# A decoder step in fp32: the second half's layer norm takes its squares about a pivot, during the output projection

## The chip, the cores and the metric

The kernel runs on one core of a Trainium2 chip. The metric is device time in microseconds of one execution, as the median of several; lower is better.

## The reference

One step of a decoder layer for 512 prompt tokens, 16 meta tokens and 8 sample tokens, model width 2048, all in float32. After an input layer norm, one projection gives queries, keys, values and a pooling input; windowed attention and causal pooling give 2048 mixed channels per token. Then:

```python
def layer_norm(x, g, b):
    mu = mean(x); var = mean((x - mu) ** 2)
    return (x - mu) * rsqrt(var + 1e-5) * g + b

mix = concat(attn_out, pool_out) @ w_o
h1  = layer_norm(ALPHA * h + mix, ln1_g, ln1_b)      # the layer norm of this change
a   = silu(h1 @ w_gate) * (h1 @ w_up)                # 44 tiles of 128 columns each
out = layer_norm(ALPHA * h1 + a @ w_down, ln2_g, ln2_b)
```

## The kernel before

**Layout.** After the attention, activations lie with channels on the 128 partitions and tokens along the free axis. The 520 tokens (8 sample, 512 prompt) are two halves of HN = 260. A value of model width is 16 blocks of 128 channels; two blocks of one half make a tile of 128 x 520, named by `k2` from 0 to 7.

**Products of split numbers.** Most matmuls take a weight as a sum of a high and a low part (fp32r) and an operand likewise, and form three products: high by high, high by low, low by high (lines 203, 204, 206). A weight is split in pieces of 128 x 512: ScalarE makes the high part (line 187), VectorE the low part (line 188). Five pieces can be held at once in this stage (`WB`). These two operations are given a priority 400 steps ahead of their place in the program (`WPRIO`).

**Output projection.** `out_proj(h)` runs over the 16 column blocks `m` of w_o for one half `h`. Each takes 48 products and four splits. Then VectorE adds ALPHA times the residual (line 858) and adds the result to `zs`, the running sum of the blocks (line 862). The result `z1[h][k2]` stays in memory.

**Layer norm.** `ln1(h, zs)` is a generator that is advanced step by step between other work. The mean over channels is one matmul of `zs` with a matrix `onesd` that holds 1/2048 everywhere (line 878), so every partition gets the sum. ScalarE copies it (line 880). Then VectorE subtracts the mean from every tile (line 892) and ScalarE squares it.

- For half 0 the squares are added on VectorE into one tile `ss` (lines 897 to 901) and two matmuls sum that over the channels (line 911). This half's norm runs beside the second half's output projection.
- For half 1 each of the 16 blocks of squares goes straight to the array, which sums them in 16 matmuls (line 888).

`rstd_of` makes the reciprocal root with one refining step (lines 238 to 244): VectorE and ScalarE in turn. Then `norm` multiplies (line 920), applies gain and offset on ScalarE (line 923) and stores h1 (line 925). For half 1, lines 934 to 949 form the differences and high and low parts (lines 871, 872) that the gate and up products need.

**Fills.** Gate and up are formed by a seven-product scheme over 2 x 2 blocks, whose first products need only half 0. While half 1's norm runs, the array takes 14 such products in plain f32, eight matmuls each (`ahead`, line 1009). Four stay in the accumulator banks; ten are copied out into the `fill` ring, a ring of five tiles of 128 x 520 (`NF`).

**Order.** A planner chooses each engine's order from a simulated timeline and the priorities. Where the code says `step(pe)`, the array's order is fixed as written: here the first half of fill 0, the mean, the second half of fill 0, the variance, and then the other fills. The steps of `rstd_of` have a priority 600 steps ahead (`LP`); so do the first nine norm steps beside the fills. Loads of weights and stores of h1 are issued from SP's queue. A fill's load needs one of five raw buffers, so it is issued when the fill five back is done.

The loop around the change, from the kernel before:

```python
    for f in (fills[0], g1, fills[0], g1):
        with step(pe):
            next(f)
    for j, f in enumerate(fills[1:]):
        with tc.high_priority(LP if j < 9 else 0):
            next(g1, None)
        with step(pe):
            for _ in f:
                pass
```

Of the kernel before, what the change touches and what calls it, by code (L numbers as in the profile page):

```python
# [8 lines left out]
F32 = mybir.dt.float32  # L9
F32R = mybir.dt.float32r  # L10
AF = mybir.ActivationFunctionType
ALU = mybir.AluOpType
AX = mybir.AxisListType

P = 128
D = 2048
# [8 lines left out]
HN = NTOK // 2  # L25
# [10 lines left out]
EPS = 1e-5  # L36
# [3 lines left out]
NF = 5  # L40
NKEEP = 2
LP = 600
# [25 lines left out]
def hybrid_step(ctx, tc, xin, w_in, w_o, w_g, w_u, w_d, w_pool, par_d, cst_d, ident_d, ln2gb, kct_d, vc_d, hist_d,  # L68
                ck_d, cv_d, sp_d, yp, ys, nkp, nvp, npp, nks, nvs, nps):
    nc = tc.nc  # L70
# [69 lines left out]
    bufs = {"raw": NRAW, "row": 16}  # L140
    par = cp.tile([P, NPAR], F32, name="par")
    onesd = cp.tile([P, P], F32, name="onesd")
# [9 lines left out]
    def row_tile(name, w=NTOK):  # L152

        return ap_.tile([P, NTOK], F32, tag="row", name=name, bufs=bufs["row"])[:, :w]
# [53 lines left out]
    def full_block(src, name, out, hi, lo, low=None, apart=False, side=None):  # L208


        def mm(w, g, js):
            for kk in range(4):
                k = g * 4 + kk
                sl = slice(kk * P, (kk + 1) * P)
                products([out[j] for j in js], w[0][:, sl], w[1][:, sl], [hi(k)[j] for j in js], [lo(k)[j] for j in js],
                         k == 0, k == KT - 1)
                if side is not None:
                    next(side)

        js = list(range(len(out)))  # L220
        ws = []
        for h in range(2):
            raw = load_raw(src[:, h * 1024:(h + 1) * 1024], f"{name}_{h}")
            for g in range(2):
                ws.append(split(raw[:, g * 512:(g + 1) * 512], f"{name}_{h}{g}", low))
                mm(ws[-1], 2 * h + g, js[:1] if apart else js)
        if apart:
            for g in range(4):
                mm(ws[g], g, js[1:])

    def rstd_of(pool, var, n, name):

        w = var.shape[-1]
        if w < HN:
            ve, r, t = [pool.tile([P, NS], F32, tag=f"rs{i}", name=f"rs{i}_{name}", bufs=3)[:n, :w] for i in range(3)]
        else:
            ve, r, t = [pool.tile([P, HN], F32, tag="r" if i == 1 else "t", bufs=1 if i == 1 else NT) for i in range(3)]
        nc.vector.tensor_scalar(ve, var, EPS, None, op0=ALU.add)
        nc.scalar.activation(t, ve, AF.Sqrt)
        nc.vector.reciprocal(r, t)  # L240
        nc.vector.tensor_mul(t, r, r)
        nc.vector.tensor_mul(t, t, ve)
        nc.vector.tensor_scalar(t, t, -0.5, 1.5, op0=ALU.mult, op1=ALU.add)
        nc.vector.tensor_mul(r, r, t)
        return r
# [5 lines left out]
    def stats_end(pool, st, mv, n, name):  # L251
        nc.vector.bn_aggr(mv[:n], st[:n].rearrange("p a b -> p (a b)"))
        return mv[:n, 0:1], rstd_of(pool, mv[:n, 1:2], n, name)
# [3 lines left out]
    with ExitStack() as sa:  # L257
# [185 lines left out]
        for h in range(2):  # L443
            for g in range(4):
                n = h * 4 + g + 1
# [27 lines left out]
            with step(*three):  # L473
                for i in range(4):
                    if i % 2:
                        nc.vector.tensor_scalar(zkv[i][:, XH[h]], out[i], par[:, PBIAS + i:PBIAS + i + 1], None,
                                                op0=ALU.add)
# [339 lines left out]
    pb, gp = Pool(fr), Pool(rr, Region("mid_b", F32R, MDW))  # L817
# [3 lines left out]
    def bank(name, w=HN):  # L821
        return ps.tile([P, 512], F32, tag="bank", name=name, bufs=banks)[:, :w]
# [15 lines left out]
    z1 = [[], []]  # L838

    def pair(d, k2, h):  # L840
        return d[2 * k2:2 * k2 + 2, :, HALF[h]].rearrange("k p c -> p k c")

    def t_tile(name):
        return pb.tile([P, 2, HN], F32, tag="t", name=name, bufs=NT)

    def out_proj(h, side=None):
        zs = pb.tile([P, HN], F32, tag="zs", bufs=2)
        for m in range(KT):
            k2, j = m // 2, m % 2
            if j == 0:  # L850
                hb = t_tile(f"hb{h}_{k2}")
                nc.sync.dma_start(hb, pair(h_d, k2, h))
                z1[h].append(row_tile(f"z1{h}_{k2}").rearrange("p (a b) -> p a b", a=2))
            out = bank(f"o{h}_{m}")
            full_block(w_o[m], f"o{h}_{m}", [out], lambda k: [mh[h][k // 2][:, k % 2, :]],
                       lambda k: [ml[h][k // 2][:, k % 2, :]])
            z = z1[h][k2][:, j, :]
            nc.vector.scalar_tensor_tensor(z, hb[:, j, :], ALPHA, out, op0=ALU.mult, op1=ALU.add)
            if m == 0:
                nc.vector.tensor_copy(zs, z)  # L860
            else:
                nc.vector.tensor_add(zs, zs, z)
            if side is not None:
                next(side, None)
        return zs
# [3 lines left out]
    def put(name, i, s):  # L869
        hi, lo = bop[name][i]  # L870
        nc.scalar.copy(hi, s)
        nc.vector.tensor_sub(lo, s, hi.bitcast(F32))

    def ln1(h, zs):


        mp = bank(f"mean{h}")
        nc.tensor.matmul(mp, onesd, zs, start=True, stop=True)
        mean = pb.tile([P, HN], F32, tag="zs", bufs=2)
        nc.scalar.copy(mean, mp)  # L880
        yield
        vp = bank(f"var{h}")
        both = lambda x: x.rearrange("p (a b) -> p a b", a=1).to_broadcast([P, 2, HN])
        sqs = []

        def var(k2):
            for j in range(2):
                nc.tensor.matmul(vp, onesd, sqs[k2][:, j, :], start=(k2 + j == 0), stop=(k2 + j == 8))

        for k2 in range(8):  # L890
            a = z1[h][k2]
            nc.vector.tensor_sub(a, a, both(mean))
            if h == 0:

                if k2 == 0:
                    ss = pb.tile([P, 2, HN], F32, tag="fill", name="ss", bufs=NF)
                    nc.scalar.activation(ss, a, AF.Square)
                else:
                    sq = t_tile(f"sq{h}_{k2}")
                    nc.scalar.activation(sq, a, AF.Square)  # L900
                    nc.vector.tensor_add(ss, ss, sq)
                if k2 % 2:
                    yield
                continue
            sqs.append(t_tile(f"sq{h}_{k2}"))
            nc.scalar.activation(sqs[k2], a, AF.Square)
            if k2:
                var(k2 - 1)
        if h == 0:
            for j in range(2):  # L910
                nc.tensor.matmul(vp, onesd, ss[:, j, :], start=(j == 0), stop=(j == 1))
        else:
            var(7)
        with tc.high_priority(LP):
            r = rstd_of(pb, vp, P, f"ln1{h}")
        yield

        def norm(k2):
            a = z1[h][k2]
            nc.vector.tensor_mul(a, a, both(r))  # L920
            for j in range(2):
                k = 2 * k2 + j
                nc.scalar.activation(a[:, j, :], a[:, j, :], AF.Identity, scale=par[:, PG1 + k:PG1 + k + 1],
                                     bias=par[:, PB1 + k:PB1 + k + 1])
            nc.sync.dma_start(pair(h1_d, k2, h), a)
            return a

        if h == 0:
            for k2 in range(8):
                put("b11" if k2 < 4 else "b21", k2 % 4, norm(k2))  # L930
                yield
            return
        for i in range(4):
            c11, c21, c12 = z1[0][i], z1[0][i + 4], norm(i)
            c22 = norm(i + 4)
            yield

            t1, t2 = t_tile(f"t1_{i}"), t_tile(f"t2_{i}")
            nc.vector.tensor_sub(t1, c12, c11)
            nc.vector.tensor_sub(t2, c22, t1)  # L940
            put("t2", i, t2)
            put("t1", i, t1)
            yield
            t3, t4 = t_tile(f"t3_{i}"), t_tile(f"t4_{i}")
            nc.vector.tensor_sub(t3, c22, c12)
            put("t3", i, t3)
            nc.vector.tensor_sub(t4, c21, t2)
            put("t4", i, t4)
            put("b22", i, c22)
            yield  # L950
# [149 lines left out]
    def staged(go, i):  # L1100
# [17 lines left out]
        for n, y in ((1, go[1]), (3, t12), (5, t34)):  # L1118
# [6 lines left out]
            yield  # L1125

    g0 = ln1(0, out_proj(0))
    zs1 = out_proj(1, g0)
    for _ in g0:
        pass  # L1130
# [4 lines left out]
    for a, b in zip(sets, sets[1:]):  # L1135
        a.next = b
    g1 = ln1(1, zs1)
    fills = [s.ahead(n) for n in (1, 2) for s in sets[:NKEEP]]
    for j, s in enumerate(sets[NKEEP + 1::2][:NFILL]):
        if j % 2 == 0:  # L1140
            f = pb.tile([P, 2, HN], F32, tag="fill", name=f"fill{j}", bufs=NF)
        fills.append(s.ahead(1, f[:, j % 2, :]))
    pe = nc.tensor
    for f in (fills[0], g1, fills[0], g1):
        with step(pe):
            next(f)
    for j, f in enumerate(fills[1:]):
# [35 lines left out]
    accp, rp, pb = Pool(fr), Pool(fr), Pool(fr)  # L1183
# [95 lines left out]
    for x, (c, j) in enumerate(pairs[2:], 2):  # L1279
# [5 lines left out]
        for i in range(5):  # L1285
# [7 lines left out]
            elif j < 2 * len(PLAIN) and i == 0:  # L1293
# [3 lines left out]
                f = j  # L1297
# [20 lines left out]
    pb, zp = Pool(fr), Pool(Region("mid_c", F32, MDW))  # L1318
# [212 lines left out]
```

## Time and profile before

| what | value |
|---|---|
| time, median of 3 runs | 1917.1 us (1916.21 to 1918.35) |
| the profiled execution's own time | 1920.76 us |
| its span, first to last instruction | 1919.0 us |
| TensorE busy | 1887.9 us, 98% of the span |
| VectorE busy | 1537.8 us, 80% |
| ScalarE busy | 957.2 us, 50% |
| mean granted TensorE clock | 0.995 |
| the second half's output projection on the array | about 440 to 532 us |
| the second half's layer norm and the fills | about 532 to 590 us |

PE is TensorE's matmuls, PEld its weight loads, DVE is VectorE, ACT is ScalarE, SP issues transfers. Times of rows are counted from the start of the span. `<-` after an idle time names the instruction that ended it.

### The profile page before, as it was taken

To read this page: it belongs to the slowest core of one execution; us is meant where nothing else is said; L and a number is where in the kernel's file an instruction comes from. 1 tells how busy PE (TensorE), PEld (TensorE's weight loads), DVE (VectorE), ACT (ScalarE), POOL (GpSimd) and SP (SyncE) were. 2 spreads that over 40 slices of the span, in tenths; PEclk is the share of its full clock that TensorE was granted. 3 is DMA by queue.
4 is the path that set the end of the run, shared out by engine and by line. 5 is a ranking of instruction groups with operands and counts; after the bars stand their busy time and mean duration, and the time that the engine had idled before them with its cause. 6 is when DMAs were issued, how large, how long until landed. Compare 5 with 4: busy or idle time off the path is not lost.

```text
span 1919.0 us, 39213 instructions
## 1 busy us (share of the span) xinstructions
PE 1887.9 (98%) x15533; PEld 1860.3 (97%) x15533; DVE 1537.8 (80%) x2734; ACT 957.2 (50%) x1808; POOL 2.7 (0%) x9
## 2 busy tenths in 40 slices
PE   8999999999999999999999999999999999999996
PEld 8999999999989999999999999999999999999996
DVE  6666667768777888988898888888878888888878
ACT  6644445545654555555555555555554433444341
POOL 0000000000000000000000000000000000000000
PEclk9999999999999999999999999999999999999998
DMA  8731222665745445454544354443568655645332
GB/s 276 234 103 63 75 73 80 208 207 191 248 154 171 156 165 176 145 188 144 172 153 168 128 168 148 156 166 127 180 245 325 232 192 183 219 164 188 95 100 90
DMA packets 145240, 319.27 MB, mean 166 GB/s; under 512 B 14288, under 2 KB 66232, under 8 KB 144952
## 3 DMA queue, kind: packets, MB, share of 16 engines
q1 hardware_dynamic: 144480, 315.71, 49.0%
q8 instruction: 122, 2.00, 0.4%
q10 hardware_dynamic: 576, 1.05, 0.2%
q14 instruction: 62, 0.51, 0.1%
HBM read 265.22 MB, written 54.03 MB: 166 GB/s over the span
## 4 chain that ended last, share of the span: by engine, by line
PE 93%; DVE 3%; ACT 2%; DMA 2%; issue 1%; SPq 0%; DVEq 0%; ACTq 0%
PE p_g L203 8%; PE p_g L204 8%; PE p_g L206 8%; PE p_u L203 7%; PE p_u L206 7%; PE p_u L204 7%; PE tri L203 6%; PE tri L206 6%; PE tri L204 6%; PE o L203 3%; PE o L206 3%; PE o L204 3%; PE p_u L1009 2%; PE mm_u L203 2%; PE mm_q L203 2%; PE mm_u L206 2%
## 5 line engine op out<-in xcount | busy, mean ns | idle before, releaser
L187 ACT CAST rr<-fr 128x512 fp32r<-128x512 f32 (+1 forms) x1056 | 669.7, 644 | 734.7 <-DVE fr L196 152.5
L188 DVE TENSOR_TENSOR rr<-fr,rr 128x512 fp32r<-128x512 f32 (+1 forms) x1056 | 744.7, 716 | 239.1 <-ACT rr L187 228.6
L196 DVE TENSOR_TENSOR fr<-fr 128x1024 f32<-128x1024 f32 (+1 forms) x304 | 319.6, 1051 | 5.0 <-DMA fr<-in_w_g_dram 4.5
L203 PE MATMUL p_g<-rr 128*128 128x260 f32 x830 | 234.1, 283 | 0.0
L206 PE MATMUL p_g<-rr 128*128 128x260 f32 x830 | 230.2, 282 | 0.0
L204 PE MATMUL p_g<-rr 128*128 128x260 f32 x788 | 221.4, 282 | 0.0
L203 PE MATMUL p_u<-rr 128*128 128x260 f32 x770 | 217.7, 283 | 0.2 <-ACT fr L1050 0.2
L206 PE MATMUL p_u<-rr 128*128 128x260 f32 x770 | 214.7, 281 | 0.0
L204 PE MATMUL p_u<-rr 128*128 128x260 f32 x748 | 210.5, 282 | 0.0
L206 PE MATMUL tri<-rr 128*128 128x260 f32 x696 | 196.8, 283 | 2.2 <-DVE rr L188 2.2
L203 PE MATMUL tri<-rr 128*128 128x260 f32 x696 | 197.1, 283 | 0.8 <-ACT rr L187 0.8
L204 PE MATMUL tri<-rr 128*128 128x260 f32 x696 | 196.7, 283 | 0.0
L203 PEld LDWEIGHTS p_g<-rr 128*128 128x128 f32 x830 | 156.1, 188 | 0.0
L206 PEld LDWEIGHTS p_g<-rr 128*128 128x128 f32 x830 | 155.1, 189 | 0.0
L204 PEld LDWEIGHTS p_g<-rr 128*128 128x128 f32 x788 | 148.1, 188 | 0.0
L203 PE MATMUL o<-rr 128*128 128x260 f32 x512 | 145.0, 284 | 0.3 <-ACT rr L187 0.3
L203 PEld LDWEIGHTS p_u<-rr 128*128 128x128 f32 x770 | 144.8, 188 | 0.4 <-ACT fr L1050 0.4
L206 PEld LDWEIGHTS p_u<-rr 128*128 128x128 f32 x770 | 144.5, 189 | 0.0
L204 PE MATMUL o<-rr 128*128 128x260 f32 x512 | 144.0, 282 | 0.0
L206 PE MATMUL o<-rr 128*128 128x260 f32 x512 | 143.6, 282 | 0.2 <-DVE rr L188 0.2
L204 PEld LDWEIGHTS p_u<-rr 128*128 128x128 f32 x748 | 140.6, 188 | 0.0
L206 PEld LDWEIGHTS tri<-rr 128*128 128x128 f32 x696 | 131.3, 189 | 3.0 <-DVE rr L188 3.0
(320 smaller groups left out, 4560.7 us busy)
## 6 DMA issues: line engine op xcount, KB each, us to landing
fr<-in_w_u_dram SPq DMA_DIRECT2D x100, 512.0 KB
fr<-in_w_g_dram SPq DMA_DIRECT2D x90, 512.0 KB
fr<-in_w_d_dram SPq DMA_DIRECT2D x64, 640.0 KB
t_d<-fr SPq DMA_DIRECT2D x140, 260.0 KB
fr<-in_w_o_dram SPq DMA_DIRECT2D x64, 512.0 KB
fr<-in_w_in_dram SPq DMA_DIRECT2D x48, 512.0 KB
rr<-t_d SPq DMA_DIRECT2D x87, 260.0 KB
mid_b<-t_d SPq DMA_DIRECT2D x53, 260.0 KB
```

Of the source, the lines that this page charges most:

```text
L187: nc.scalar.copy(wh, s)
L188: last_lo[0] = (lo or nc.vector).tensor_sub(wl, s, wh.bitcast(F32)).ins
L196: i = op(*args).ins
L203: nc.tensor.matmul(o, wh, hi[j], start=first, stop=False, skip_group_check=onto)
L204: nc.tensor.matmul(o, wh, lo[j], start=False, stop=False, skip_group_check=onto)
L206: nc.tensor.matmul(o, wl, hi[j], start=False, stop=last, skip_group_check=onto)
L1009: nc.tensor.matmul(bk, self.q(0, n - 1)[:, k * P:(k + 1) * P], z1[0][4 * (n - 1) + k // 2][:, k % 2, :], start=(k == 0), stop=(k == 7))
```

## The change

Half 1's squares are now formed while its output projection still runs, about a pivot instead of the mean. After column block 8, one matmul of the running sum `zs` and a copy on ScalarE with a factor 2048/(9 x 128) give the mean of the first nine blocks, per token: the pivot. From block 9 on, VectorE subtracts the pivot from the blocks that are finished (in place), ScalarE squares them, and VectorE adds the squares into a tile `ss1`. Blocks 9, 10 and 11 are followed by one pair of blocks each, 12 and 13 by two pairs each, 14 and 15 by themselves. The square of block 15 stays apart.

Behind the projection the array takes the mean, the two halves of `ss1` and the square of block 15: four matmuls in place of seventeen. The mean becomes the mean minus the pivot (`mean`); its square (`less`) is subtracted from the variance in `rstd_of`, in the operation that adds the epsilon. `norm` first subtracts `mean` from each tile of half 1. The tiles of the `fill` ring hold pivot, `ss1`, squares and `less` at fixed places, and the fills' copies are given places that fit. `ln1(1)` has one step fewer, so the array's written order becomes: first half of fill 0, mean and variance, second half of fill 0, the other fills. Half 0 is as before.

```diff
+    def fill_tile(name, at):
+        return pb.tile([P, 2, HN], F32, tag="fill", name=name, bufs=NF, at=at)
+
+    both = lambda x: x.rearrange("p (a b) -> p a b", a=1).to_broadcast([P, 2, HN])
+    pivot, ss1, sq1 = [], [], []
+
+    def shift(m, zs):
+        def square(a, name, at):
+            nc.vector.tensor_sub(a, a, both(p) if len(a.shape) > 2 else p)
+            sq = fill_tile(name, at)
+            sq = sq if len(a.shape) > 2 else sq[:, 0, :]
+            nc.scalar.activation(sq, a, AF.Square)
+            return sq
+
+        if m == 8:
+            pp = bank("pivot")
+            nc.tensor.matmul(pp, onesd, zs, start=True, stop=True)
+            pivot.append(fill_tile("pivot", 0)[:, 0, :])
+            nc.scalar.activation(pivot[0], pp, AF.Copy, scale=D / (9.0 * P))
+            ss1.append(fill_tile("ss1", 1))
+        if m < 9:
+            return
+        p, ss = pivot[0], ss1[0]
+        for k2 in {9: (0,), 10: (1,), 11: (2,), 12: (3, 4), 13: (5, 6)}.get(m, ()):
+            sq = square(z1[1][k2], f"sq1_{k2}", 2 + k2 % 3 if k2 else 1)
+            if k2:
+                nc.vector.tensor_add(ss, ss, sq)
+        if m >= 14:
+            sq = square(z1[1][7][:, m % 2, :], f"sq1_{m}", 4 if m == 14 else 3)
+            if m == 14:
+                nc.vector.tensor_add(ss[:, 0, :], ss[:, 0, :], sq)
+            else:
+                sq1.append(sq)
...
     def out_proj(h, side=None):
...
                 nc.vector.tensor_add(zs, zs, z)
+            if h:
+                shift(m, zs)
...
     def rstd_of(pool, var, n, name, less=None):
...
+        if less is None:
+            nc.vector.tensor_scalar(ve, var, EPS, None, op0=ALU.add)
+        else:
+            nc.vector.scalar_tensor_tensor(ve, var, EPS, less, op0=ALU.add, op1=ALU.subtract)
...
     def ln1(h, zs):
...
-            sqs.append(t_tile(f"sq{h}_{k2}"))
-            nc.scalar.activation(sqs[k2], a, AF.Square)
-            if k2:
-                var(k2 - 1)
...
-            var(7)
+            for j in range(2):
+                nc.tensor.matmul(vp, onesd, ss1[0][:, j, :], start=(j == 0), stop=False)
+            nc.tensor.matmul(vp, onesd, sq1[0], start=False, stop=True)
+            with tc.high_priority(LP):
+                nc.vector.tensor_sub(mean, mp, pivot[0])
+                less = fill_tile("less", 4)[:, 0, :]
+                nc.scalar.activation(less, mean, AF.Square)
         with tc.high_priority(LP):
-            r = rstd_of(pb, vp, P, f"ln1{h}")
+            r = rstd_of(pb, vp, P, f"ln1{h}", less)
...
         def norm(k2):
             a = z1[h][k2]
+            if h:
+                nc.vector.tensor_sub(a, a, both(mean))
             nc.vector.tensor_mul(a, a, both(r))
...
-            f = pb.tile([P, 2, HN], F32, tag="fill", name=f"fill{j}", bufs=NF)
+            f = fill_tile(f"fill{j}", (2 + j // 2) % NF)
...
-    for f in (fills[0], g1, fills[0], g1):
+    for f in (fills[0], g1, fills[0]):
```

More of the change, by code (lines that the diff above doesn't have):

```diff
@@ L229, in full_block, with rstd_of @@
                 mm(ws[g], g, js[1:])
-    def rstd_of(pool, var, n, name):
+    def rstd_of(pool, var, n, name, less=None):
         w = var.shape[-1]
@@ L237, in rstd_of @@
             ve, r, t = [pool.tile([P, HN], F32, tag="r" if i == 1 else "t", bufs=1 if i == 1 else NT) for i in range(3)]
-        nc.vector.tensor_scalar(ve, var, EPS, None, op0=ALU.add)
+        if less is None:
+            nc.vector.tensor_scalar(ve, var, EPS, None, op0=ALU.add)
+        else:
+            nc.vector.scalar_tensor_tensor(ve, var, EPS, less, op0=ALU.add, op1=ALU.subtract)
         nc.scalar.activation(t, ve, AF.Sqrt)
@@ L879, in ln1 @@
         mean = pb.tile([P, HN], F32, tag="zs", bufs=2)
-        nc.scalar.copy(mean, mp)
-        yield
         vp = bank(f"var{h}")
[L883 to L893, printed above, removed]
+        less = None
+        if h == 0:
+            nc.scalar.copy(mean, mp)
+            yield
+            for k2 in range(8):
+                a = z1[h][k2]
+                nc.vector.tensor_sub(a, a, both(mean))
                 if k2 == 0:
-                    ss = pb.tile([P, 2, HN], F32, tag="fill", name="ss", bufs=NF)
+                    ss = fill_tile("ss", 0)
                     nc.scalar.activation(ss, a, AF.Square)
@@ L903, in ln1 @@
                     yield
-                continue
-            sqs.append(t_tile(f"sq{h}_{k2}"))
-            nc.scalar.activation(sqs[k2], a, AF.Square)
-            if k2:
-                var(k2 - 1)
-        if h == 0:
             for j in range(2):
@@ L919, in norm @@
             a = z1[h][k2]
+            if h:
+                nc.vector.tensor_sub(a, a, both(mean))
             nc.vector.tensor_mul(a, a, both(r))
```

## The prediction

> **What bounds the kernel now.** I read the page first: the busy shares of the engines (us, share of the span, instructions) and the chain that ended last.
>
> ```profile
> PE 1887.9 (98%) x15533; PEld 1860.3 (97%) x15533; DVE 1537.8 (80%) x2734; ACT 957.2 (50%) x1808; POOL 2.7 (0%) x9
> ...
> PE 93%; DVE 3%; ACT 2%; DMA 2%; issue 1%; SPq 0%; DVEq 0%; ACTq 0%
> ```
>
> TensorE is the bound: a matmul taken out is worth its time on the array, unless a neighbour then waits. Second, what the array waited for between 440 and 600 us, which holds the second half's output projection and layer norm (us in total, times, longest):
>
> ```profile
> PE o L203 <- ACT rr L187: 0.3, 1, 0.3
> PE o L206 <- DVE rr L188: 0.2, 1, 0.2
> ```
>
> Both waits are for the splits of w_o; no matmul waits on the layer norm, because the fills lie over its chain. So an earlier norm buys nothing by itself: only array time counts. Third, the timeline around the norm (start us, us, engine, line, output and input, count):
>
> ```profile
> 532.60 0.43 DVE L858 SCALAR_TENSOR_TENSOR fr<-fr,o 128x260 f32<-128x260 f32 x1 [4.86 <-PE o L206]
> 533.06 0.43 DVE L862 TENSOR_TENSOR fr<-fr 128x260 f32<-128x260 f32 x1
> ...
> 534.15 0.60 PE L878 MATMUL mean<-fr 128*128 128x260 f32 x2
> ...
> 534.59 1.91 PE L1009 MATMUL p_g<-fr 128*128 128x260 f32 x8
> 534.79 0.38 ACT L880 COPY fr<-mean 128x260 f32<-128x260 f32 x1 [8.87 <-PE mean L878]
> 535.20 4.97 DVE L892 TENSOR_TENSOR fr<-fr 128x520 f32<-128x520 f32 x8 [1.71 <-ACT fr L880]
> 535.93 2.56 ACT L906 ACTIVATE fr<-fr 128x520 f32<-128x520 f32 x4 [0.77 <-DVE fr L892]
> ...
> 536.62 7.31 PE L888 MATMUL var<-fr 128*128 128x260 f32 x32
> ...
> 543.77 3.67 PE L1009 MATMUL p_u<-fr 128*128 128x260 f32 x16
> 544.04 0.43 DVE L238 TENSOR_SCALAR fr<-var 128x260 f32<-128x260 f32 x1 [3.87 <-PE var L888]
> ...
> 547.27 3.67 PE L1009 MATMUL p_g<-fr 128*128 128x260 f32 x16
> ...
> 548.03 0.43 DVE L244 TENSOR_TENSOR fr<-fr 128x260 f32<-128x260 f32 x1
> 548.50 3.75 DVE L920 TENSOR_TENSOR fr<-fr 128x520 f32<-128x520 f32 x6
> ```
>
> An f32 matmul of the program shows as two array instructions: a fill's eight are x16. The spacing of starts is the real price: 543.77 to 547.27 is 3.50 us for 16, 0.219 us each, 0.44 us for one matmul. The single duration (3.67 for the group, about 0.38 for one) overlaps its neighbour.
>
> **What goes.** The fill's half of 8 instructions starts at 534.59 and would hand over at 534.59 + 8 x 0.219 = 536.34. The next fill starts at 543.77. So the sixteen variance matmuls take 7.43 us of the array (16 x 0.44 = 7.0, the rest hand-over to the first square).
>
> **What comes on the array.** Three variance matmuls behind the mean: 3 x 0.44 = 1.32 us. One pivot matmul in the projection: 0.44. The mean's matmul stays. Gross saving 7.43 - 1.32 - 0.44 = 5.67 us.
>
> [...] I stay with the spacing of starts, since that is what the next fill waits for.
>
> **Must the three matmuls wait for their operands?** They follow the mean directly and would start at about 534.59, 535.03 and 535.47. The last reads the square of column block 15: its z and zs are done at 533.06 + 0.43 = 533.49, a half-width subtraction takes 0.43 (L862), its square about 0.38 (L880, the same width on ScalarE), two hand-overs about 0.1 each: ready at 534.5, a microsecond before its turn. No wait.
>
> **The work put into the projection.** VectorE gets seven full subtractions at 4.97/8 = 0.62 us, two half ones at 0.43, six full additions at 0.62 and one half at 0.43: 9.35 us, in blocks 9 to 15. ScalarE gets one pivot copy (0.38), seven full squares (0.64) and two half ones: 5.6 us. How full both are there (span, us long, then PE, PEld, DVE, ACT busy):
>
> ```profile
> 490.00:495.00 5.00, 4.48 (x37) 4.06 (x35) 3.70 (x7) 5.00 (x11) 0.00 (x0) 1.00 0.96 288
> 495.00:500.00 5.00, 5.00 (x40) 4.86 (x41) 4.73 (x9) 5.00 (x11) 0.00 (x0) 1.00 1.03 325
> 500.00:505.00 5.00, 5.00 (x45) 5.00 (x44) 5.00 (x10) 2.77 (x5) 0.00 (x0) 1.00 0.83 270
> 505.00:510.00 5.00, 5.00 (x44) 5.00 (x43) 3.24 (x6) 2.36 (x4) 0.00 (x0) 1.00 0.77 243
> 510.00:515.00 5.00, 5.00 (x44) 5.00 (x43) 3.01 (x6) 1.98 (x4) 0.00 (x0) 1.00 0.73 266
> 515.00:520.00 5.00, 5.00 (x44) 5.00 (x44) 2.99 (x6) 2.31 (x4) 0.00 (x0) 1.00 0.53 153
> 520.00:525.00 5.00, 5.00 (x44) 5.00 (x44) 3.33 (x6) 2.04 (x4) 0.00 (x0) 1.00 0.60 202
> 525.00:530.00 5.00, 5.00 (x45) 5.00 (x43) 1.75 (x4) 0.62 (x1) 0.00 (x0) 1.00 0.58 191
> 530.00:535.00 5.00, 5.00 (x34) 4.67 (x33) 0.86 (x2) 0.21 (x1) 0.00 (x0) 1.00 0.04 16
> ```
>
> From 505 to 535 VectorE is busy 15.2 of 30 us, so 14.8 are free for the 9.35, and ScalarE has far more. The cover is this idle time, and the lead of the splits, which have priority:
>
> ```profile
> 501.41 3.09 DVE L188 TENSOR_TENSOR rr<-fr,rr 128x512 fp32r<-128x512 f32 x5
> ...
> 525.95 0.69 DVE L188 TENSOR_TENSOR rr<-fr,rr 128x512 fp32r<-128x512 f32 x1 [0.74 <-ACT rr L187]
> 526.85 0.42 DVE L858 SCALAR_TENSOR_TENSOR fr<-fr,o 128x260 f32<-128x260 f32 x1 [0.20 <-PE o L206]
> ```
>
> Block 15 ends just before 532.60 and is 532.60 - 526.85 = 5.75 long, a quarter of it 1.44. Its last split is done at 526.64 and used from about 531.0: a lead of 4.3 us. At 501.41 that lead is gone: five splits stand back to back, and both waits of the array above fall at 494 to 495, with ScalarE full. Only two items of the change reach into this stretch with their full weight: the pivot after block 8 (491.37 in the next fence) and the first subtraction and square after block 9.
>
> ```profile
> 491.37 0.43 DVE L858 SCALAR_TENSOR_TENSOR fr<-fr,o 128x260 f32<-128x260 f32 x1 [0.43 <-PE o L206]
> ...
> 492.32 0.42 DVE L862 TENSOR_TENSOR fr<-fr 128x260 f32<-128x260 f32 x1
> ```
>
> The pivot matmul needs zs at 492.74. Placed straight behind block 8 it would hold the array 492.74 + 0.2 - 491.3 = 1.6 us; placed once zs is ready, nothing. The planner decides; I take 0.1, with 0 to 1.6 as bounds. The copy (0.38), the subtraction (0.62) and the square (0.64) may come ahead of a late split: 0 to 1.6 us, and I take 0.4, since the splits have priority but no lead there. A changed order could also mend what this stretch loses now: 37 and 40 instructions in the first two rows against 44 is 11 x 0.12 = 1.3 us to win.
>
> The nearest precedent is the first half's norm, which put the same kind of work into the same loop. Groups of instructions, 444 to 474 us (busy us, mean ns, idle before):
>
> ```profile
> L203 PE MATMUL o<-rr 128*128 128x260 f32 x81 | 23.3, 288 | 0.0
> ...
> L892 DVE TENSOR_TENSOR fr<-fr 128x520 f32<-128x520 f32 x8 | 5.0, 692 | 0.0
> L901 DVE TENSOR_TENSOR fr<-fr 128x520 f32<-128x520 f32 x7 | 4.9, 695 | 0.0
> L900 ACT ACTIVATE fr<-fr 128x520 f32<-128x520 f32 x7 | 4.5, 636 | 0.1
> L911 PE MATMUL var<-fr 128*128 128x260 f32 x4 | 1.0, 382 | 0.0
> ```
>
> Eight subtractions, eight squares and seven additions lay there beside the splits, with the norm's own variance matmuls in the stream, and the array idled 0.0 us.
>
> **Behind the sums.** Variance is ready at 534.59 + 1.32 = 535.9, against 543.9 before. The normaliser's chain keeps its length: 544.04 to 548.46, 4.4 us; its first step only becomes a three-operand one, like L858 (0.42). The mean minus pivot and its square (0.42 and 0.38) run beside the variance matmuls. So r comes at about 540.4, 8 us earlier, while the fills run 5.7 earlier. VectorE then has eight more subtractions, 5.0 us. Its norm work lasts now to 577.03 + 0.70, 29.2 us from 548.50:
>
> ```profile
> 550.78 38.74 PE L1009 MATMUL p_u<-fr 128*128 128x260 f32 x176
> ...
> 577.03 0.70 DVE L872 TENSOR_TENSOR mid_b<-fr,mid_b 128x520 fp32r<-128x520 f32 x1
> ...
> 582.84 1.22 DVE L196 TENSOR_TENSOR fr<-fr 128x1024 f32<-128x1024 f32 x1 [4.32 <-DMA fr<-in_w_g_dram]
> ```
>
> After: 540.4 + 29.2 + 5.0 = 574.6. The next VectorE work, the first weight sum, waits for a load that the fills release, so it moves with them to 582.84 - 5.7 = 577.1, and the fills end at 589.5 - 5.7 = 583.8. The margin shrinks from 5.1 to 2.5 us and costs nothing; even if gone, the first product starts another 6.7 us later. The eight stores of h1 and the fills' loads share SP's queue as before, in the same counts: a load is five buffers, four fills of 3.5 us, ahead.
>
> **Sum.** 5.67 - 0.1 - 0.4 = 5.2 us, 0.27%. The profiled execution is 1920.8 us (span 1919.0 and 1.8 around it), 3.7 above the median of 1917.1; so 1915.6 against it, and against the median 1911.9. What is unknown gives the likeliest case 5.67 + 1.3 = 7.0 to 5.67 - 1.6 - 1.6 = 2.5: 1910.1 to 1914.6.
>
> **The rivals.** (1) Given back in the crowded stretch. The gain goes where the splits have no lead: both bounds together, 3.2 us, leave 2.5: 1914.6; with a microsecond or two more of disturbed order later on, up to 1917. For it: ScalarE at 5.00 of 5.00 from 490 to 500. Against it: the priority of the splits and the precedent.
>
> (2) Slower: VectorE stands still for the squares. Each addition needs a square that ScalarE makes between it and its subtraction. If the planner puts them next to each other, VectorE waits 0.64 + 0.1 per column pair, and as long again where the square stands behind a cast that waits for the array. Eight times 0.74 to 1.5 on top of 9.35 is 15 to 21 us. From 505 to 525 VectorE has 20 - 12.6 = 7.4 us free, and the lead gives 4.3: 11.7 together. The array then waits up to 9.6 us, and the time is 1917.1 - 5.7 + 9.6 = 1921.0. It decides from (11.7 + 5.7 - 9.35)/8 = 1.0 us of standing still per pair. Against it: L901 in the first half, 7 additions with 0.0 idle before them.
>
> (3) The saving is not there: the mean and three sums wait for late squares, say with VectorE's backlog from blocks 12 and 13, which take two pairs each. The array then idles behind the fill's half, up to the 5.67. VectorE needs 4 x 0.62 = 2.5 us more in each of those blocks and has 5.75 x (1 - 3.1/5) = 2.2; the 4.86 us of idle before L858 at 532.60 take up the rest. 1917.
>
> **How the numbers follow.** No change can be told from 0.2%, 3.8 us, either way: 1913.3 to 1920.9. Likeliest case 0.66, nearly all of it below 1913.3; rival 1, 0.15; rival 3, 0.06; rival 2, 0.08; a shift of order further on that costs more than all this, 0.05. Faster 0.64, same 0.23, slower 0.13. The range reaches from the best order, 1910.0, over rivals 1 and 3 to 1918.5; the likeliest case alone is 1910.1 to 1914.6.
>
> **What would show it.** Right: mean and variance as eight array instructions in one run, ahead of the first fill's second half; the array's waits from 440 to 600 at about 0.5 us to 1.5; the last fill ending 5 us earlier; every later stage of unchanged length. Wrong: waits of L203 or L206 on L187 or L188 in blocks 9 to 13 (rivals 1, 2), an idle L901-like addition with ScalarE as releaser (2), the variance matmuls behind a gap (3), or a wait of the first products on t3.

## The result, and the profile after

The change makes the kernel faster, by about half of what was forecast: the median is 1915.8 us of 20 runs (1912.7 to 1917.7) against 1918.1 us of 20 runs of the kernel before (1916.2 to 1920.1). The ratio is 0.9986 with a 95% interval of 0.9980 to 0.9993, a gain of 1.3 to 3.8 us, best value 2.7. The forecast was 5.2 us; its range held the time. The likeliest case of the prediction ran from 2.5 to 7.0 us of gain, so 2.7 lies at its lower edge. Measured against the 0.2% that the prediction set, a gain of 0.14% counts as "same" (chance 0.23 there) and not as "faster" (0.64); the interval, narrower than 0.2%, tells it from no change.

The page of the changed kernel first, busy shares and chain:

```profile
PE 1882.2 (98%) x15509; PEld 1856.3 (97%) x15509; DVE 1546.3 (81%) x2751; ACT 956.4 (50%) x1810; POOL 2.7 (0%) x9
...
PE 91%; DVE 3%; DMA 3%; ACT 1%; issue 1%; SPq 0%; DVEq 0%; ACTq 0%
```

The array has 24 instructions fewer, which is twelve matmuls, and is still the bound. What it waited for between 440 and 600 us is new:

```profile
PE pivot L867 <- DVE fr L901: 1.5, 1, 1.5
PE o L206 <- DVE rr L188: 1.1, 1, 1.1
```

Before, there were 0.5 us of waits; now there are 2.6. The first is the new matmul itself: the pivot waits for the running sum. The timeline around the norm answers to the one of before (start us, us, engine, line, count):

```profile
533.05 0.43 DVE L897 SCALAR_TENSOR_TENSOR fr<-fr,o 128x260 f32<-128x260 f32 x1 [3.48 <-PE o L206]
...
534.60 0.60 PE L919 MATMUL mean<-fr 128*128 128x260 f32 x2
535.04 1.04 PE L942 MATMUL var<-fr 128*128 128x260 f32 x4
535.24 0.43 DVE L945 TENSOR_TENSOR fr<-mean,fr 128x260 f32<-128x260 f32 x1 [0.84 <-PE mean L919]
535.71 4.97 DVE L955 TENSOR_TENSOR fr<-fr 128x520 f32<-128x520 f32 x8
535.92 0.60 PE L943 MATMUL var<-fr 128*128 128x260 f32 x2
536.36 1.92 PE L1045 MATMUL p_g<-fr 128*128 128x260 f32 x8
...
544.58 0.43 DVE L247 TENSOR_TENSOR fr<-fr 128x260 f32<-128x260 f32 x1
...
574.31 0.70 DVE L913 TENSOR_TENSOR rr<-fr,rr 128x520 fp32r<-128x520 f32 x1 [0.16 <-ACT rr L912]
578.58 1.23 DVE L196 TENSOR_TENSOR fr<-fr 128x1024 f32<-128x1024 f32 x1 [3.57 <-DMA fr<-in_w_g_dram]
583.51 0.48 PE L203 MATMUL p_g<-mid_b,rr 128*128 128x260 f32 x1
```

Mean and variance are eight array instructions in one run, and the fill goes on right behind them. To compare two executions I use two stretches, both marked by rows of their own: from the addition behind block 8 to the addition behind block 15 (the projection), and from there to the first gate product (norm and fills). The marks of before are 491.37 and 532.60, shown in the prediction, and this row:

```profile
589.16 0.48 PE L203 MATMUL p_g<-mid_b,rr 128*128 128x260 f32 x1
```

The marks of the changed kernel are 533.05 and 583.51 above and 488.89 in the next fence.

| stretch | before | after | difference | forecast |
|---|---|---|---|---|
| block 8 to block 15 | 41.23 | 44.16 | +2.93 | +0.94 |
| block 15 to the first gate product | 56.56 | 50.46 | -6.10 | -6.11 |
| both | 97.79 | 94.62 | -3.17 | -5.17 |

The norm gives what was worked out, to 0.01 us. The projection costs three times what was allowed. The 3.2 us left agree with the measured 2.7 (1.3 to 3.8). The profiled spans differ by more, 1919.0 against 1914.1: in these two executions the first half's mean starts at 443.66 and 441.42 us. Up to the pivot both kernels issue the same instructions in the same order on the array, so that 2.2 us belongs to the executions and not to the change. 1.4 us of it are there by 25 us from the start: the array waits 2.03 us at 17 us in the first and 0.41 us in the second. Another 1.1 us come at 340 us, where the granted clock was 0.50 in the first and 1.00 in the second; 0.2 us go the other way at 51 us. Windows of before at 340 us, then of the changed kernel (span, us long, PE, PEld, DVE, ACT, POOL busy with counts, granted clock, DMA share, GB/s):

```profile
340.29:343.70 3.41, 3.41 (x28) 2.80 (x24) 3.41 (x13) 3.19 (x9) 0.00 (x0) 0.50 0.87 265
```

```profile
340.29:343.70 3.41, 3.41 (x30) 3.03 (x27) 3.41 (x10) 2.43 (x7) 0.00 (x0) 1.00 0.90 247
```

Where the projection loses time, in rows of VectorE, ScalarE and the array of the changed kernel, in order of time:

```profile
488.89 0.43 DVE L897 SCALAR_TENSOR_TENSOR fr<-fr,o 128x260 f32<-128x260 f32 x1 [0.19 <-PE o L206]
489.24 0.68 DVE L188 TENSOR_TENSOR rr<-fr,rr 128x512 fp32r<-128x512 f32 x1
489.84 0.42 DVE L901 TENSOR_TENSOR fr<-fr 128x260 f32<-128x260 f32 x1
490.32 0.71 PE L867 MATMUL pivot<-fr 128*128 128x260 f32 x2 [1.46 <-DVE fr L901]
...
495.52 0.38 ACT L869 ACTIVATE fr<-pivot 128x260 f32<-128x260 f32 x1
496.68 1.30 DVE L859 TENSOR_TENSOR fr<-fr 128x520 f32<-128x520 f32 x2
497.90 0.42 DVE L897 SCALAR_TENSOR_TENSOR fr<-fr,o 128x260 f32<-128x260 f32 x1
498.24 1.30 DVE L859 TENSOR_TENSOR fr<-fr 128x520 f32<-128x520 f32 x2
499.45 0.68 DVE L188 TENSOR_TENSOR rr<-fr,rr 128x512 fp32r<-128x512 f32 x1
500.19 0.39 PE L206 MATMUL o<-rr 128*128 128x260 f32 x1 [1.14 <-DVE rr L188]
```

The pivot's matmul stands in the array's order straight behind block 8. Its sum is ready only after the addition L897, a split that has priority (L188), and L901, so every product of block 9 stands behind it. When the pivot has reached memory, VectorE takes four subtractions (L859) at once, not the one that is written after block 9. The split at 499.45 comes behind them, and the array waits for it.

### The profile page after: what moved, and what is told of

The parts are those of the page before. It is cut to its first block, busy times and chain, and to the rows that moved or that the text cites. A ratio compares the mean times of both kernels' runs of the same rounds, so it can differ in the third digit from the quotient of the medians.

```text
span 1914.1 us, 39184 instructions
## 1 busy us (share of the span) xinstructions
PE 1882.2 (98%) x15509; PEld 1856.3 (97%) x15509; DVE 1546.3 (81%) x2751; ACT 956.4 (50%) x1810; POOL 2.7 (0%) x9
## 4 chain that ended last, share of the span: by engine, by line
PE 91%; DVE 3%; DMA 3%; ACT 1%; issue 1%; SPq 0%; DVEq 0%; ACTq 0%
PE p_g L203 8%; PE p_g L204 8%; PE p_g L206 8%; PE p_u L203 7%; PE p_u L204 7%; PE p_u L206 7%; PE tri L203 6%; PE tri L206 6%; PE tri L204 6%; PE o L203 3%; PE o L206 3%; PE o L204 3%; PE p_u L1045 2%; PE mm_u L203 2%; PE mm_q L203 2%; PE mm_u L206 2%
## 5 line engine op out<-in xcount | busy, mean ns | idle before, releaser
L188 DVE TENSOR_TENSOR rr<-fr,rr 128x512 fp32r<-128x512 f32 (+1 forms) x1056 | 743.8, 715 | 234.3 <-ACT rr L187 223.8
L206 PE MATMUL p_g<-rr 128*128 128x260 f32 x830 | 230.5, 282 | 0.0
L206 PE MATMUL p_u<-rr 128*128 128x260 f32 x770 | 214.9, 282 | 0.0
L206 PE MATMUL tri<-rr 128*128 128x260 f32 x696 | 196.9, 283 | 1.7 <-DVE rr L188 1.7
L206 PEld LDWEIGHTS p_g<-rr 128*128 128x128 f32 x830 | 155.2, 189 | 0.0
L206 PE MATMUL o<-rr 128*128 128x260 f32 x512 | 143.8, 282 | 1.1 <-DVE rr L188 1.1
L206 PEld LDWEIGHTS p_u<-rr 128*128 128x128 f32 x770 | 144.6, 189 | 0.0
L206 PEld LDWEIGHTS tri<-rr 128*128 128x128 f32 x696 | 131.4, 189 | 2.5 <-DVE rr L188 2.5
```

The lines of the kernel that those rows point to most:

```text
L188: last_lo[0] = (lo or nc.vector).tensor_sub(wl, s, wh.bitcast(F32)).ins
L206: nc.tensor.matmul(o, wl, hi[j], start=False, stop=last, skip_group_check=onto)
```

## The experiments

Theory A: the saving on the array is real, and the missing part is lost in two waits of the projection that the change itself makes. Theory B: array time saved around the norm is given back in later stages. Each comparison is with the kernel before on the same chip.

**The pivot inside block 9.** Theory A says that its wait is a matter of its place in the array's order.

```diff
+    def make_pivot(zs):
+        for _ in range(5):
+            yield
+        pp = bank("pivot")
+        nc.tensor.matmul(pp, onesd, zs, start=True, stop=True)
...
-        if m == 8:
-            pp = bank("pivot")
-            nc.tensor.matmul(pp, onesd, zs, start=True, stop=True)
...
-                       lambda k: [ml[h][k // 2][:, k % 2, :]])
+                       lambda k: [ml[h][k // 2][:, k % 2, :]],
+                       side=make_pivot(zs) if (h, m) == (1, 9) else None)
```

> The pivot's matmul is emitted after a third of block 9's products, not between blocks 8 and 9; all else as in the change. Theory A (the array loses the missing gain in two waits of its own: 1.5 us for zs in front of the pivot, 1.1 us for a split behind the early subtractions): the wait in front of the pivot goes to 0, from the end of block 8 to the end of block 15 it takes 1.5 us less (42.7 instead of 44.2), ratio to the kernel before about 0.9975. Theory B (array time saved around the norm is given back in later stages, whatever happens in the projection): the wait goes, the time stays at a ratio of 0.9986.

Ratio 0.9978 (0.9970 to 0.9987), which holds the values of both theories (0.9975 and 0.9986); the rows have to tell. The wait in front of the pivot is gone, but the projection takes 43.18 us (42.7 was expected), only 1.0 less than with the change. The rest moved into the other wait. Rows of this kernel, VectorE and the array:

```profile
498.02 1.92 DVE L870 TENSOR_TENSOR fr<-fr 128x520 f32<-128x520 f32 x3
...
500.19 0.69 DVE L870 TENSOR_TENSOR fr<-fr 128x520 f32<-128x520 f32 x1
...
502.15 0.39 PE L206 MATMUL o<-rr 128*128 128x260 f32 x1 [1.72 <-DVE rr L188]
```

L870 is the subtraction here. Without the pause at the pivot the array runs ahead, and meets the late split with 1.7 us of wait in place of 1.1. The two waits are not independent: time lost at the first gives the splits a part of their lead back.

**The pivot and the pairs later.**

```diff
-        if m == 8:
+        if m == 10:
...
-            nc.scalar.activation(pivot[0], pp, AF.Copy, scale=D / (9.0 * P))
+            nc.scalar.activation(pivot[0], pp, AF.Copy, scale=D / (11.0 * P))
...
-        if m < 9:
+        if m < 11:
...
-        for k2 in {9: (0,), 10: (1,), 11: (2,), 12: (3, 4), 13: (5, 6)}.get(m, ()):
+        for k2 in {11: (0, 1), 12: (2, 3), 13: (4, 5), 14: (6,)}.get(m, ()):
```

> The pivot is taken after block 10 (mean of eleven blocks), its matmul still between two blocks; the pairs follow blocks 11 to 14. Theory A: the crowded stretch up to 505 us is left alone, so the wait of 1.1 us on the low part of a split goes; the wait in front of the pivot stays, 0.9 to 1.5 us; end of block 8 to end of block 15 about 43.0 us, ratio about 0.9978. Theory B: ratio 0.9986. A third theory, that VectorE has no room for the work wherever it lies: new waits on low parts of splits in blocks 11 to 14, ratio 0.9986 or above.

Ratio 0.9987 (0.9978 to 0.9996), where theory A had 0.9978 and theory B 0.9986, and the projection takes 45.51 us, more than with the change (43.0 was expected). The waits are as theory A has them: nothing new for the splits, and 2.0 us in front of the pivot (0.9 to 1.5 were expected).

```profile
PE pivot L867 <- DVE fr L901: 2.0, 1, 2.0
PE o L203 <- ACT rr L187: 0.3, 1, 0.3
PE o L206 <- DVE rr L188: 0.2, 1, 0.2
```

But 41.23 + 0.44 + 2.0 is 43.7, and 1.8 us are unaccounted for. The windows of this kernel show them:

```profile
502.00:504.00 2.00, 0.37 (x1) 0.37 (x2) 1.58 (x4) 0.15 (x1) 0.00 (x0) 0.92 0.83 283
504.00:506.00 2.00, 2.00 (x9) 1.81 (x9) 0.68 (x2) 0.39 (x1) 0.00 (x0) 0.50 0.61 223
506.00:508.00 2.00, 2.00 (x14) 2.00 (x14) 2.00 (x5) 1.93 (x4) 0.00 (x0) 0.73 0.45 176
508.00:510.00 2.00, 2.00 (x19) 2.00 (x18) 2.00 (x4) 2.00 (x4) 0.00 (x0) 1.00 0.00 0
```

The array's granted clock fell to 0.50 behind the wait, from 503.68 to 507.09. It is busy all the time there, with 9 and 14 instructions in 2 us where it otherwise makes 19: (10 + 5) x 0.12 = 1.8 us. So the ratio is theory B's number for a reason that is not theory B's. Only one execution of this kernel was profiled, the longest of 11 (1917.5; median 1916.2, shortest 1914.9); whether the clock falls in each of them is not shown.

**Both edits.** The pivot is taken from eleven blocks, inside block 11, and the pairs follow blocks 11 to 14.

```diff
-        for k2 in {9: (0,), 10: (1,), 11: (2,), 12: (3, 4), 13: (5, 6)}.get(m, ()):
+        for k2 in {11: (0, 1), 12: (2, 3), 13: (4, 5), 14: (6,)}.get(m, ()):
...
+                       side=make_pivot(zs) if (h, m) == (1, 11) else None)
```

> Both edits: pivot from the first eleven blocks, its matmul after a third of block 11's products, pairs after blocks 11 to 14. Theory A: both waits go, end of block 8 to end of block 15 about 41.7 us (41.2 of before and 0.44 for the matmul), the whole gain of 5.7 us arrives: ratio 0.9970. Theory B: ratio 0.9986.

Ratio 0.9967 (0.9954 to 0.9979). The projection takes 41.67 us: 41.23 and 0.44 for the pivot's matmul, to the digit. Waits of the array from 440 to 600 us, and the two marks on VectorE:

```profile
PE o L203 <- ACT rr L187: 0.3, 1, 0.3
PE o L206 <- DVE rr L188: 0.2, 1, 0.2
```

```profile
488.51 0.43 DVE L903 SCALAR_TENSOR_TENSOR fr<-fr,o 128x260 f32<-128x260 f32 x1 [0.43 <-PE o L206]
...
530.18 0.42 DVE L903 SCALAR_TENSOR_TENSOR fr<-fr,o 128x260 f32<-128x260 f32 x1 [2.93 <-PE o L206]
```

These are the waits of before and no others. Both stretches together are 92.12 us, 5.67 less than before: the gross saving of the prediction. Theory A stands and theory B falls: its 0.9986 lies outside the interval.

**Twelve matmuls put back.** The other side of the question: does array time around the norm count in full?

```diff
             nc.tensor.matmul(vp, onesd, sq1[0], start=False, stop=True)
+            more = bank("more")
+            for j in range(12):
+                nc.tensor.matmul(more, onesd, sq1[0], start=(j == 0), stop=(j == 11))
```

> The change with twelve more f32 matmuls of the same size behind the variance's last, into a bank of their own that nobody reads. Theory A (time on the array around the norm counts in full): 12 x 0.44 = 5.3 us slower than the change, so 2 us slower than the kernel before, ratio about 1.0011; the stretch from fill 0 to the first gate product goes from 50.7 to 56.0 us. Theory B: under 3 us slower than the change, ratio below 1.0002.

Ratio 1.0008 (0.9999 to 1.0017), 1.0011 expected. From block 15 to the first gate product it takes 55.72 us, 5.26 more than the change. The added group in this kernel's timeline:

```profile
535.90 5.42 PE L946 MATMUL more<-fr 128*128 128x260 f32 x24
541.16 1.92 PE L1048 MATMUL p_g<-fr 128*128 128x260 f32 x8
```

541.16 - 535.90 = 5.26 us for 24 instructions, 0.219 each. Time on the array counts in full there.

**No pivot at all.** If an early norm buys nothing, half 1 can be done as half 0 was: mean, subtractions, squares summed on VectorE, two matmuls, all behind the projection.

```diff
-            if h == 0:
+            if True:
                 if k2 == 0:
                     ss = pb.tile([P, 2, HN], F32, tag="fill", name="ss", bufs=NF)
...
-        else:
-            var(7)
...
-    for f in (fills[0], g1, fills[0], g1):
+    for f in (fills[0], g1, fills[0]):
         with step(pe):
             next(f)
+    with tc.high_priority(LP):
+        next(g1)
+    for f in fills[1:4]:
+        with step(pe):
+            for _ in f:
+                pass
+    with step(pe):
+        next(g1)
-    for j, f in enumerate(fills[1:]):
+    for j, f in enumerate(fills[4:]):
```

> The kernel before with half 1's norm done as half 0's: mean first, then eight subtractions, eight squares and seven additions on VectorE and ScalarE behind the projection, and two variance matmuls in place of sixteen, placed behind fill 3; no pivot, nothing put into the projection. Theory A (only array time and the array's own waits count): fourteen matmuls and the hand-over go, 14 x 0.44 + 0.4 = 6.6 us, no wait in the projection beyond the 0.5 us of before; VectorE's norm work ends some 4 us later against the fills and is still covered: ratio 0.9966. Rival (the norm's chain must come early, which is why the squares were moved): the first gate product waits for its operands or for its split, ratio 0.998 or above, with a wait of the array on VectorE behind the last fill.

Ratio 0.9988 (0.9980 to 0.9997): here the rival was right. The stretch to the first gate product is 50.01 us, 6.55 less than before, as expected. Then the cover runs out:

```profile
PE p_g L206 <- DVE rr L188: 0.7, 1, 0.7
PE p_g L203 <- ACT mid_b L871: 0.5, 1, 0.5
PE p_g L203 <- ACT fr L1032: 0.5, 1, 0.5
```

The first gate products wait 1.7 us, for their operands (L871), a split (L188) and a copy. From the first gate product to the first product of the down projection this kernel takes 849.8 us where the one of before takes 847.2. In the 15 us around that first product VectorE has no idle time here (577.80 to 592.80), while the kernel of before has it busy 12.55 of 15 (584.16 to 599.16). So the additions that were left behind the projection fall into a stretch in which VectorE is the next thing to be late. That the lateness of the norm itself costs nothing is not shown: the wait for L871 can come from either. Nor do the stretches account for all: 6.55 less 2.6 is 3.9 us, where the ratio says 2.3 (0.6 to 3.8).

As it stands, the change is no faster than this simpler kernel (0.9986 against 0.9988). With both edits it is, by the first measurement, whose interval (0.9954 to 0.9979) ends below that of this one; that of the second (0.9959 to 0.9983) overlaps it.

**Which of the two edits holds the subtractions back?** This kernel is the one with the pivot inside block 9, from nine blocks, with the pairs written later.

```diff
-        for k2 in {9: (0,), 10: (1,), 11: (2,), 12: (3, 4), 13: (5, 6)}.get(m, ()):
+        for k2 in {11: (0, 1), 12: (2, 3), 13: (4, 5), 14: (6,)}.get(m, ()):
```

> The pivot from nine blocks with its matmul inside block 9, as in e1, but the pairs written after blocks 11 to 14, as in e3. Theory A1 (the subtractions go when the pivot is there, wherever they are written): four subtractions before 502 us ahead of the splits, the array waits 1.9 us on low parts as in e1, end of block 8 to end of block 15 about 43.2 us. Theory A2 (the place in the program holds them back): no such wait, 41.7 us as in e3.

A1: the projection takes 43.19 us, and the wait and the early subtractions are those of the first experiment. There is one run of it, 1914.0 us, too few for a verdict on the time. Waits of the array and two rows of VectorE:

```profile
PE o L206 <- DVE rr L188: 1.9, 2, 1.7
```

```profile
498.86 1.91 DVE L870 TENSOR_TENSOR fr<-fr 128x520 f32<-128x520 f32 x3
501.04 0.69 DVE L870 TENSOR_TENSOR fr<-fr 128x520 f32<-128x520 f32 x1
```

A place further down in the program does not hold work back in this profile; a pivot that is ready later does, as the kernel with both edits shows.

**The change and the best version again, on one chip.**

> The change itself once more, beside the next run on the same chip: ratio 0.9983 by theory A (5.7 us less 2.5 us of waits in the projection), end of block 8 to end of block 15 44.2 us.

> The kernel of e3 once more: ratio 0.9970 by theory A, 2.5 us less than the change on the same chip; end of block 8 to end of block 15 41.7 us.

The change: ratio 0.9982 (0.9973 to 0.9990), projection 44.16 us. Pivot and pairs later: 0.9971 (0.9959 to 0.9983), projection 41.68 us. The stretches differ by 2.5 us again, as expected. The times differ by 2.1 us in the ratio's best values, with intervals that overlap; both pairs of runs point the same way.

The two stretches and the ratios can now be set side by side, as gains in us: 4.2 and 4.2 with the pivot inside, 1.8 and 2.5 with pivot and pairs later, 5.7 and 6.3 with both edits (5.7 and 5.6 the second time), -2.1 and -1.5 with twelve more, 3.2 and 3.5 for the change again. They agree to 0.7 us, so as far as the intervals allow (1 us and more to each side), what these kernels gain or lose lies in these two stretches.

**The wait lengthened.** The extra 1.8 us of the later pivot came with a lower clock. Is it the wait that lowers it? Copies of the sum on VectorE make the pivot's operand later: one copy in the first kernel, as in the diff, and four in the second.

```diff
         if m == 8:
             pp = bank("pivot")
+            for i in range(1):
+                zc = fill_tile(f"zc{i}", 2 + i % 2)[:, 0, :]
+                nc.vector.tensor_copy(zc, zs)
+                zs = zc
             nc.tensor.matmul(pp, onesd, zs, start=True, stop=True)
```

> The change with one copy of zs on VectorE (about 0.3 us) between the running sum and the pivot's matmul, which reads the copy: the array's wait in front of the pivot grows from 1.5 to 1.8 us. Theory C (what cost extra in e2 is the clock that falls to one half after a wait of about 2 us): just under or at that length, so either the clock stays at 1.00 and the end of block 8 to the end of block 15 takes 44.5 us, or it falls and takes 46.2. Theory D (the clock fell in e2 for a reason of its own): 44.5 us, clock 1.00.

> The same with four copies in a chain: the wait grows to about 3 to 3.5 us, well past the 2.0 of e2. Theory C: the granted clock falls to 0.50 for some 3.4 us behind the pivot and the matmuls there start 0.22 us apart, as in e2; from the end of block 8 to the end of block 15 about 47.7 us, of which 1.7 from the clock. Theory D: clock 1.00 throughout, about 46.0 us.

Theory C holds for the clock. With one copy the wait is 1.8 us, and the clock is 0.50 from 490.77, just behind it, to 494.18. With four it is 3.3 us, and the clock is 0.50 from 490.26, while the array still waits (until 491.60), to 497.08. Windows of the kernel with one copy, then of the one with four:

```profile
490.00:492.00 2.00, 1.41 (x5) 1.22 (x6) 1.27 (x4) 2.00 (x5) 0.00 (x0) 0.69 1.02 347
492.00:494.00 2.00, 2.00 (x11) 2.00 (x11) 1.67 (x3) 2.00 (x5) 0.00 (x0) 0.50 1.10 362
```

```profile
492.00:494.00 2.00, 2.00 (x9) 1.81 (x9) 1.67 (x4) 2.00 (x5) 0.00 (x0) 0.50 1.07 368
494.00:496.00 2.00, 2.00 (x11) 2.00 (x11) 2.00 (x4) 2.00 (x6) 0.00 (x0) 0.50 1.02 324
```

The length of the projection does not tell the theories apart: 44.43 us is what theory D had for one copy (44.5; theory C 46.2 with a lower clock), and 46.66 for four lies between the two (46.0 and 47.7). The wait of 1.1 us on a split vanished in both, probably because the slower array let the splits catch up. Each kernel ran once (1914.7 and 1915.3 us, 1919.8 for the one of before), which gives no verdict on the time.

## Why the prediction was right or wrong

Right, by its own steps:

- The price of a matmul by the spacing of starts, and with it 7.43 us out and 1.32 in: the stretch shrank by 6.10 us where 6.11 was worked out, and twelve put back cost 5.26. Counted by the busy time of their weight loads instead, 24 of 0.19 us (the next row, of the fills of before), the twelve would cost 4.6 us; the run agrees with the spacing.

```profile
L1009 PEld LDWEIGHTS p_u<-fr x192: 188/190/190, 543.5 to 588.9; 128*128 128x128 f32 x192
```

- No wait of the three matmuls for their squares: mean and variance run from 534.60 to 536.36 without a gap. Rival 3 did not happen.
- Nothing gained by the earlier norm itself, and nothing lost behind it: VectorE's norm work ended at 574.31 + 0.70 = 575.0 (574.6 was worked out), the first weight sum at 578.58 still waited for its load. The way there was another: the eight new subtractions (L955) went ahead of the reciprocal root, at 535.71, so the root came at 544.58 + 0.43 = 545.0 and not at 540.4, and the sum of the work was the same. That 575.0 lies so near to 574.6 is luck in part: the order that gave it was not the one foreseen.
- Rival 2 did not happen: VectorE stood idle in front of three of the additions for their squares, but for 0.1, 0.1 and 0.5 us, behind 513 us, and the array did not wait there.

Wrong were two terms of the sum, both in the crowded stretch. Their bounds held (0 to 1.6 us each); the values taken inside them did not:

- "Placed straight behind block 8 it would hold the array 1.6 us; placed once zs is ready, nothing." The row put the planner's choice on the first: 1.46 us. The prediction works out no ground for the 0.1 that it took; its nearest support is the first half's precedent, and that does not bear: the first half's mean was written behind a whole further block of products, so its operand was old when its turn came. The pivot was written straight behind the block that completes its operand.
- "Only two items of the change reach into this stretch with their full weight." Four subtractions did, 2.6 us of VectorE, because they depend on the pivot and on blocks that were done long before. The step took the place in the program for the time of execution. The array waited 1.1 us, where 0.4 was taken. This is the sign that the prediction had named for rival 1: a wait of L206 on L188 in blocks 9 to 13 (block 10, at 500.19), and 2.6 us of waits in all where it allowed 0.5 to 1.5.

Together the projection cost 2.93 us and not 0.94. That is the bound of rival 1, "both bounds together, 3.2 us": gain 2.5 worked out there, 3.2 in the stretches, 2.7 in the time. So what came is rival 1 (chance 0.15), and the range held the time because it had been drawn wide enough for it. The idle 14.8 us of VectorE were a true cover for all that lay behind 505 us, as the kernel with both edits shows, but an average over 30 us said nothing about the 10 us in which the splits had no lead.

## What to carry to other kernels

A matmul whose operand another engine finishes last should be written some way behind it (a third of a block was enough here), not straight behind it: the array takes its instructions in the planned order, and everything behind it waits too. Under a planner like this one, work that is moved under a cover may start as soon as its operands are ready, not where it is written: ask for each moved instruction when its last operand comes, and what stands on its engine then. If that moment is a crowded one, delay the operand.

## What the runs showed of the hardware

A short wait of the array can cost twice. With waits of 1.8, 2.0 and 3.3 us in front of the pivot the granted clock was 0.50 for 3.4, 3.4 and 6.8 us (from 490.77, 503.68 and 490.26; the third began 1.3 us before its wait ended), with products 0.22 us apart in place of 0.12. Other waits left the clock at 1.00: 1.46 us (the change, twice, and the kernel with twelve more matmuls), and 1.72 us in the two kernels with the pivot inside block 9. Such a window of the second of these, at whose middle the wait ends (502.99):

```profile
502.00:504.00 2.00, 1.01 (x8) 1.01 (x9) 2.00 (x4) 0.83 (x2) 0.00 (x0) 1.00 0.13 22
```

That is not a threshold between 1.72 and 1.8 us: the length of the wait alone does not decide. The change was profiled twice, and near the start of both executions the same matmul waits equally long. A wait and the window behind it in the first:

```profile
48.36 0.30 PE L371 MATMUL xt<-fr,mid_a 128*128 128x128 f32 x1 [1.27 <-DVE fr L377]
...
50.64:54.05 3.41, 3.41 (x16) 3.41 (x17) 2.84 (x5) 2.32 (x5) 0.00 (x0) 0.50 0.34 112
```

and the same in the second, where the clock stayed:

```profile
48.90 0.30 PE L371 MATMUL xt<-fr,mid_a 128*128 128x128 f32 x1 [1.26 <-DVE fr L377]
...
50.64:54.05 3.41, 3.27 (x24) 2.81 (x23) 3.00 (x5) 2.38 (x5) 0.00 (x0) 1.00 0.26 84
```

And at 340 us in the kernel of before it was 0.50 for 3.4 us with no wait of the array ahead of it. What else decides whether the clock falls, no run here separates.

The Trainium skill, page "TensorE: Matmul & The Clock Gate", section "What's actually happening", has the clock halved after at least one idle window of about 3.4 us; here waits of 1.8 and 2.0 us were enough in two of the three kernels.
